# Weight chunks in the order of use, masks written by VectorE, and squares added by TensorE in a three-layer transformer kernel

## The chip, the cores and the metric

The kernel runs on one core of one Trainium2 chip. The metric is the device time of one execution in microseconds. The core's engines are named as the profile names them: PE (TensorE matmul) and PEld (its weight load), DVE (VectorE), ACT (ScalarE), POOL (GpSimd) and SP (SyncE, which issues most DMAs).

## The reference

A sequence of 256 tokens of width 1024 goes through one block with two kinds of softmax attention and then through two blocks with two feed-forward stages each, a mixer between them (retention in the first, stick-breaking attention in the second) and a gated embedding at the end. Everything is float32. Cut to what the change touches:

```python
def rms_norm(x, w):                       # also on the latents cq (384 wide) and ckv (256 wide)
    return x * rsqrt(mean(x * x, -1) + 1e-6) * w

def chunk_causal_attention(q, k, v, scale):     # 8 heads of one kind (two scores each), 8 of the other
    mask = key_chunk[None, :] <= q_chunk[:, None]      # chunks of 64 tokens, query blocks of 128
    sc = where(mask, einsum('bhqd,bhkd->bhqk', qi, k) * scale, -1e30)
    return softmax(sc) @ v

def stick_breaking(h, w_in, w_out):             # 8 heads, strictly causal
    z = q @ k.T * scale
    log_one_minus = where(kpos < qpos, log_sigmoid(-z), 0)
    rem = reversed_cumsum(log_one_minus) - log_one_minus
    a = where(kpos < qpos, exp(log_sigmoid(z) + rem), 0)
    return (a @ v) @ w_out

# the end of each of the two later blocks
gate = sigmoid(rmsnorm(h, g[6]) @ ple_w_gate[i])
h = h + rmsnorm(gate * (p[i] @ ple_w_proj[i]), g[7])
```

## The kernel before

**Precision.** Each float32 product with a weight is made of three products of rounded parts. `chunk` loads up to 2,048 columns of weights with one DMA into `w_raw`, ACT rounds each piece of 512 columns into `w_hi` (L191) and DVE writes the rest into `w_lo` (L192). There are twelve buffers of each. `mm3` (L200) then issues hi by hi, lo by hi and hi by lo. Activations lie in SBUF as a pair of the same kind (`x_hi`, `x_lo`, or `a_hi`, `a_lo` in the second half of a feed-forward stage), with features on the partitions.

**Weights by tokens.** In `tokens` a tile of 128 features by 128 tokens is the stationary operand and 512 weight columns stream past it. `parts` are the (usually two) column ranges, `groups` the runs of k (tiles of 128 features) that are worked off together, and `b` the two halves of 128 tokens. The loops run over group, b, part j, k. The chunks, though, are laid out with k outside and the part inside, so that the pieces of a group of four k stand as k0 j0, k0 j1, k1 j0, k1 j1 in the first chunk, and k2 and k3 in the second. All feed-forward stages, the output projections and the embedding's gate go this way. The other way round (`mat_steps`, L217), with weights stationary, serves the heads' projections.

**Heads.** In the first block the score matmuls of a head, its transposes and its value products stand between slices of other projections; numbers such as `FILL_DA` say how many filler matmuls go between. A scheduler orders the instructions of each engine within this, by priorities and by the lines `issue_after`. In `scores`, matmuls with a single-row operand `masks` (L665: `q0` is one for the first 64 queries, `k1` is -1e30 for the keys that they must not see) open the accumulation of each score tile S, and the products of q and k add to it (L672). A differential head has two tiles S with 64 rows of q and k each; the other kind of head (MLA) has one, from 128 rows `k,q` and 64 rows `kr,qr`. `softmax` then reads each S with a maximum on DVE (L682) and an exponential on ACT (L690). `ot` (L857) are the transposes of the preceding differential head's output, which depend on its normalisation on POOL and DVE.

**Latents.** `sumsq` adds the squares of the latents' tiles (three for cq, two for ckv): ACT squares, POOL adds into `acc` (L291), and two matmuls per latent with a column of ones sum `acc` over the partitions (L294).

**Stick-breaking.** `sums` builds reversed cumulative sums in `c` by six matmuls with `tri_r` and `ones_r`, and adds the mask by two more, `ident_r` by `neg_r` (L1218, L1221). DVE scales S into `zs` (L1199), and later adds c (L1222).

**Gated embedding.** `ple_gate` runs `tokens` over eight k in the groups `[0..3]` and `[4..7]`. When the last group's half b is done, ACT takes a tanh `z` (L1298), DVE multiplies into `e` (L1300), `residual` squares, scales by `r` (POOL, L302) and adds into `h` (L421). The next stage begins with `features`: PE transposes h into `xt` (L435), ACT and DVE write `x_hi` and `x_lo` (L439, L441). The line `issue_after(self.turn_at)` holds those transposes back until three `mm3` are left of the half that is being issued (`TURN_AT`). The first of the two embedding stages is followed by a feed-forward stage, the second ends the kernel.

Of the kernel before, what the change touches and what calls it, by code (L numbers as in the profile page):

```python
# [10 lines left out]
F32 = mybir.dt.float32  # L11
# [3 lines left out]
ALU = mybir.AluOpType  # L15
# [49 lines left out]
K_ID, K_F1, K_F2, NK = 0, 128, 129, 130  # L65
K_TRI, K_M01, K_NEG, NKS = 0, 128, 256, 384


def constants():

    i = np.arange(P)
    c = np.zeros((P, NK), np.float32)
    c[:, K_ID : K_ID + P] = np.eye(P)
    m = np.zeros((1, 4 * P), np.float32)
    m[0, :P] = i < 64
    for at in (192, 448):
        m[0, at : at + 64] = NEG
# [6 lines left out]
    t[:, K_NEG : K_NEG + P] = np.where(i[:, None] >= i[None, :], NEG, 0.0)  # L84
# [10 lines left out]
    return c, t, d, m  # L95

# [51 lines left out]
class Build:  # L148
# [93 lines left out]
    def tokens(self, parts, X, nk, banks, groups, before=(None, None)):  # L242

        width = sum(len(cols) for *_, cols in parts)
        starts = np.cumsum([0] + [len(cols) for *_, cols in parts]).tolist()
        per = CHUNK // width
        for g in groups:
            at = {}  # L250
            for i in range(0, len(g), per):
                W = self.chunk([(name, lead, k, cols) for k in g[i : i + per] for name, lead, cols in parts])
                at.update({k: (W, x * width) for x, k in enumerate(g[i : i + per])})
            for b in range(2):
                if g is groups[0] and before[b] is not None:
                    before[b]()
                left = len(parts) * len(g)
                for j, (*_, cols) in enumerate(parts):
                    for k in g:
                        left -= 1  # L260
                        W, c = at[k]
                        x = tuple(t[:, k, b * P : (b + 1) * P] for t in X)
                        self.mm3(banks[b][j], x, W(c + starts[j], len(cols)), k == groups[0][0], k == groups[-1][-1])
# [17 lines left out]
    def sumsq(self, n, tile):  # L281

        nc = self.nc
        ss = self.psa.tile([P, 2], F32, name="ss", tag="a")
        acc = self.tmp.tile([P, T], F32, name="acc", tag="acc", bufs=1)
        for i in range(n):
            src = tile(i)
            sq = acc if i == 0 else self.tmp.tile([P, T], F32, name="sq", tag="sq")
            nc.scalar.activation(sq, src, AF.Square)
            if i:  # L290
                nc.gpsimd.tensor_add(acc, acc, sq)  # L291
            yield i, src
        for b in range(2):
            nc.tensor.matmul(  # L294
                ss[:, b : b + 1], acc[:, b * P : (b + 1) * P], self.ones[:, 0:1],
                start=b == 0, stop=b == 1, skip_group_check=True,
            )
        self.ss = ss
# [242 lines left out]
    def setup_scores(self):  # L541
        nc, const, aps = self.nc, self.const, self.aps
        mk = self.tmp.tile([1, 4 * P], F32, name="mk", tag="sq")
        nc.gpsimd.dma_start(mk, aps["mk"])
        masks = self.rounded(const, "masks", mk)
        self.q0, self.k1 = masks[:, 0:P], masks[:, P:]

# [111 lines left out]
    def scores(self, Ss, parts):  # L659
# [3 lines left out]
        with self.at_pe():  # L663
            for S in Ss:
                mm(S, self.q0, self.k1, start=True, stop=False, skip_group_check=True)  # L665
            for b in range(2):
                at = slice(0, P) if b == 0 else slice(P, 3 * P)
                qs, ks = slice(b * P, (b + 1) * P), slice(0, (b + 1) * P)
                for n in range(len(parts[0])):
                    for S, qk in zip(Ss, parts):  # L670
                        q, k = qk[n]
                        mm(S[:, at], q[:, qs], k[:, ks], start=False, stop=n == len(parts[0]) - 1, skip_group_check=True)  # L672

    def softmax(self, Ss, scale):
# [4 lines left out]
        mx = self.sm.tile([P, 4], F32, name="mx", tag="mx", bufs=3)  # L679
        for e, S in enumerate(Ss):  # L680
            for b in range(2):
                nc.vector.tensor_reduce(mx[:, 2 * e + b : 2 * e + b + 1], S[:, cols[b]], axis=AX.X, op=ALU.max)  # L682
# [472 lines left out]
    def stick(self, X, R, before, row):  # L1155
        nc, tc = self.nc, self.tc
        spec = lambda c0: ("sb_w_in_2", (0,), range(c0, c0 + P))
        with tc.tile_pool(name="stick", bufs=1) as sp:
# [30 lines left out]
            def scores(h):  # L1189
# [8 lines left out]
                nc.scalar.activation(u, u, AF.Exp, scale=-1.0)  # L1198
                nc.vector.tensor_scalar_mul(zs, S, SB_SCALE)  # L1199
                nc.scalar.activation(u, u, AF.Ln, bias=1.0)  # L1200
# [8 lines left out]
            def sums(h):  # L1209
# [3 lines left out]
                with self.at_pe():  # L1213
                    mm(c[:, 0 : 2 * P], tri_r, lhi[:, 0 : 2 * P], start=True, stop=False)
                    mm(c[:, 0 : 2 * P], tri_r, llo[:, 0 : 2 * P], start=False, stop=False)
                    mm(c[:, P : 2 * P], ones_r, lhi[:, 2 * P :], start=False, stop=False)
                    mm(c[:, P : 2 * P], ones_r, llo[:, 2 * P :], start=False, stop=False)
                    mm(c[:, 0:P], ident_r, neg_r, start=False, stop=True)  # L1218
                    mm(c[:, 2 * P :], tri_r, lhi[:, 2 * P :], start=True, stop=False)
                    mm(c[:, 2 * P :], tri_r, llo[:, 2 * P :], start=False, stop=False)  # L1220
                    mm(c[:, 2 * P :], ident_r, neg_r, start=False, stop=True)  # L1221
                nc.vector.tensor_add(zs, zs, c)  # L1222
# [61 lines left out]
    def ple_gate(self, i, X, R, before, e, row, out):  # L1284
# [114 lines left out]
```

## Time and profile before

| | |
|---|---|
| median of three runs | 1623.23 us (1621.54 to 1623.61) |
| the profiled execution | 1622.01 us, its span 1620.2 us |
| PE busy | 1606.6 us, 99% of the span |
| DVE, ACT, POOL busy | 1061.3, 904.0, 90.1 us |
| granted TensorE clock, mean | 0.997 |
| DMA | 288.60 MB, mean 178 GB/s |

The rows of the profile read so: line of the kernel, engine, operation, output<-inputs, output and input shapes, count, then busy time and the mean duration of one in ns, then the engine's idle time before them and what ended it. A row of the timeline begins with the start and the duration in us; rows of equal instructions that follow each other are merged with a count, and idle time stands in brackets. A matmul's duration contains its way through the array, which overlaps the next one: what a matmul costs in a full stream is the distance from its start to the next start. A float32 matmul that isn't a transpose shows as two instructions, and the program's order below shows it as one.

### The profile page before, as it was taken

The numbers are of one execution on the slowest core, as the hardware profiler recorded it, in microseconds if no ns is written. First come the engines' busy times: TensorE is split into PE (matmuls) and PEld (weight loads), VectorE is DVE, ScalarE is ACT, GpSimd is POOL, SyncE is SP. The second block draws the span as 40 slices with busy tenths as digits, with TensorE's granted clock in tenths as the row PEclk, the third lists the DMA queues.
The fourth block names the chain that finished last, engine by engine and source line by source line (L and its number), as shares of the span: only waits on it lengthen the run. The fifth ranks groups of instructions, "written<-read, shape, count | busy, mean of one in ns | idle before, by whom it ended". The sixth has DMA issues, their size and how long they took to land.

```text
span 1620.2 us, 22387 instructions
## 1 busy us (share of the span) xinstructions
PE 1606.6 (99%) x8258; PEld 1349.5 (83%) x8258; DVE 1061.3 (66%) x1948; ACT 904.0 (56%) x1792; POOL 90.1 (6%) x101
## 2 busy tenths in 40 slices
PE   9999999999999999999999999999999999999997
PEld 9898778888888888898888888878888899888886
DVE  7987656755556555777766565576655677666546
ACT  7655544755455554645546555475554656655545
POOL 1100000200002000100000000030000200000002
PEclk9999999999999999999999999999999999999999
DMA  7535435555545555455455555555555453555451
GB/s 254 211 122 180 161 104 195 195 182 186 184 175 208 187 177 195 168 187 178 164 190 178 188 180 193 190 195 182 182 182 182 172 191 134 178 182 182 182 184 64
DMA packets 46862, 288.60 MB, mean 178 GB/s; under 512 B 5968, under 2 KB 9168, under 8 KB 13856
## 3 DMA queue, kind: packets, MB, share of 16 engines
q1 hardware_dynamic: 44240, 279.29, 48.7%
q0 software_dynamic: 2080, 7.67, 1.4%
q8 instruction: 65, 1.06, 0.3%
q14 instruction: 45, 0.37, 0.1%
q10 hardware_dynamic: 432, 0.20, 0.0%
HBM read 284.65 MB, written 1.05 MB: 176 GB/s over the span
## 4 chain that ended last, share of the span: by engine, by line
PE 95%; DVE 2%; DMA 1%; issue 1%; ACT 1%; SPq 0%; POOL 0%; POOLq 0%; DVEq 0%; ACTq 0%
PE ps L200 78%; PE ps L217 9%; PE at L638 1%; PE S L672 1%; PE xt L435 1%; DMA w_raw<-in_w 1%; DVE w_lo L192 1%; PE o L200 1%; PE o L713 0%; PE S L665 0%; PE S L1079 0%; PE S L1195 0%; DMA h<-in_x 0%; PE pt L703 0%; PE o L840 0%
## 5 line engine op out<-in xcount | busy, mean ns | idle before, releaser
L192 DVE TENSOR_TENSOR w_lo<-w_raw,w_hi 128x512 fp32r<-128x512 f32 x1054 | 707.5, 687 | 363.9 <-ACT w_hi L191 360.2
L191 ACT CAST w_hi<-w_raw 128x512 fp32r<-128x512 f32 x1054 | 638.7, 621 | 482.7 <-PE ps L200 355.3
L200 PE MATMUL ps<-w_hi,x_hi 128*128 128x512 f32 (+1 forms) x1280 | 489.4, 382 | 1.1 <-ACT x_hi L439 1.1
L200 PE MATMUL ps<-w_hi,x_lo 128*128 128x512 f32 (+1 forms) x1280 | 483.5, 378 | 1.2 <-DVE x_lo L441 1.2
L200 PE MATMUL ps<-w_lo,x_hi 128*128 128x512 f32 (+1 forms) x1280 | 482.4, 377 | 0.0
L200 PEld LDWEIGHTS ps<-w_hi,x_lo 128*128 128x128 f32 x1280 | 241.1, 188 | 47.3 <-DVE x_lo L441 2.4
L200 PEld LDWEIGHTS ps<-w_hi,x_hi 128*128 128x128 f32 x1280 | 241.3, 188 | 43.9 <-ACT x_hi L439 1.5
L200 PEld LDWEIGHTS ps<-w_lo,x_hi 128*128 128x128 f32 x1280 | 241.4, 189 | 42.0
L200 PE MATMUL ps<-w_hi,a_hi 128*128 128x512 f32 x440 | 176.8, 402 | 0.0
L200 PE MATMUL ps<-w_hi,a_lo 128*128 128x512 f32 x440 | 173.4, 394 | 0.0
L200 PE MATMUL ps<-w_lo,a_hi 128*128 128x512 f32 x440 | 172.6, 392 | 0.0
L302 POOL TENSOR_TENSOR r<-v,mhalf 128x1 f32<-128x1 f32 (+1 forms) x50 | 63.7, 1274 | 1239.8 <-DVE v L390 1100.6
L217 PE MATMUL ps<-x_hi,w_hi 128*128 128x256 f32 x440 | 114.7, 289 | 0.2 <-DVE h L780 0.2
L217 PE MATMUL ps<-x_hi,w_lo 128*128 128x256 f32 x440 | 112.5, 284 | 0.0
L200 PEld LDWEIGHTS ps<-w_hi,a_lo 128*128 128x128 f32 x440 | 82.6, 188 | 21.4
L200 PEld LDWEIGHTS ps<-w_lo,a_hi 128*128 128x128 f32 x440 | 82.7, 188 | 19.1
L200 PEld LDWEIGHTS ps<-w_hi,a_hi 128*128 128x128 f32 x440 | 82.7, 188 | 18.3
L217 PEld LDWEIGHTS ps<-x_hi,w_hi 128*128 128x128 f32 x440 | 84.1, 191 | 1.3 <-issue 0.7
L217 PEld LDWEIGHTS ps<-x_hi,w_lo 128*128 128x128 f32 x440 | 84.2, 192 | 0.6 <-DVE w_lo L192 0.3
L217 PE MATMUL ps<-x_lo,w_hi 128*128 128x256 f32 x440 | 77.5, 283 | 0.0
L633 DVE SCALAR_TENSOR_TENSOR a<-ps,R,s 128x512 f32<-128x512 f32 (+1 forms) x60 | 42.2, 703 | 52.2 <-PE ps L200 44.6
L274 ACT CAST a_hi<-at 128x512 fp32r<-128x512 f32 (+1 forms) x60 | 33.1, 552 | 67.9 <-PE at L638 67.9
(282 smaller groups left out, 1506.1 us busy)
## 6 DMA issues: line engine op xcount, KB each, us to landing
w_raw<-in_w SPq DMA_DIRECT2D x256, 1024.0 KB, 4.8
gr<-in_rows POOLq DMA_DIRECT2D x10, 512.0 KB, 4.6
w_raw<-in_w SPq DMA_DIRECT2D x12, 256.0 KB, 4.9
w_raw<-in_w SPq DMA_DIRECT2D x6, 384.0 KB, 3.2
w_raw<-in_w SPq DMA_DIRECT2D x3, 512.0 KB, 3.6
h<-in_x SPq DMA_DIRECT2D x4, 256.0 KB, 4.9
h<-in_x POOLq DMA_DIRECT2D x1, 1024.0 KB, 7.9
out<-h SPq DMA_DIRECT2D x3, 256.0 KB, 2.5
```

Source lines behind the costliest of these rows:

```text
L191: nc.scalar.copy(hi[:, :m], r[:, c0:c1])
L192: nc.vector.tensor_sub(lo[:, :m], r[:, c0:c1], hi[:, :m].bitcast(F32))
L200: mm = lambda a, b, **k: nc.tensor.matmul(ps, a, b, skip_group_check=True, **k)
L217: mm = lambda *a, **k: self.nc.tensor.matmul(*a, skip_group_check=True, **k)
L274: nc.scalar.copy(hi, src)
L302: self.nc.gpsimd.tensor_tensor(r, v, self.mhalf[:, :n], op=ALU.pow)
L435: nc.tensor.transpose(pt[:, i, :], self.h[:, b, k * P : (k + 1) * P], self.ident)
L633: nc.vector.scalar_tensor_tensor(a, banks[1], R[:, b : b + 1], s, op0=ALU.mult, op1=ALU.mult)
L638: nc.tensor.transpose(pt[:, i, :], a[:, i * P : (i + 1) * P], self.ident)
L672: mm(S[:, at], q[:, qs], k[:, ks], start=False, stop=n == len(parts[0]) - 1, skip_group_check=True)
```

## The change

It has four parts.

1. `tokens` lays a group's chunks out by part and then k, which is the order in which the matmuls use them.
2. The embedding's gate takes its eight k as three and five.
3. The masks leave PE. In the softmax heads the first product of q and k opens the accumulation, and a DVE memset (`masked`) writes -1e30 into the two 64 by 64 squares of S before the maximum is taken. In the stick-breaking heads the mask comes into `zs` where DVE scales S, from a constant that is now 384 columns wide, and the two matmuls with `neg_r` go.
4. `sumsq` keeps the squares of all tiles of a latent, and PE adds them: two matmuls for each tile instead of two for the sum. POOL's additions go.

```diff
     # tokens
-        width = sum(len(cols) for *_, cols in parts)
-        per = CHUNK // width
+        per = CHUNK // len(parts[0][2])
         for g in groups:
-            at = {}
-            for i in range(0, len(g), per):
-                W = self.chunk([(name, lead, k, cols) for k in g[i : i + per] for name, lead, cols in parts])
-                at.update({k: (W, x * width) for x, k in enumerate(g[i : i + per])})
+            at, order = {}, [(j, k) for j in range(len(parts)) for k in g]
+            for i in range(0, len(order), per):
+                part = order[i : i + per]
+                W = self.chunk([(*parts[j][:2], k, parts[j][2]) for j, k in part])
+                at.update({jk: (W, x * len(parts[0][2])) for x, jk in enumerate(part)})
     # sumsq
-        acc = self.tmp.tile([P, T], F32, name="acc", tag="acc", bufs=1)
+        sq = self.tmp.tile([P, 3, T], F32, name="sqs", tag="acc", bufs=1)
         for i in range(n):
             src = tile(i)
-            sq = acc if i == 0 else self.tmp.tile([P, T], F32, name="sq", tag="sq")
-            nc.scalar.activation(sq, src, AF.Square)
-            if i:
-                nc.gpsimd.tensor_add(acc, acc, sq)
+            nc.scalar.activation(sq[:, i, :], src, AF.Square)
             yield i, src
...
+        for i in range(n):
+            for b in range(2):
+                nc.tensor.matmul(
+                    ss[:, b : b + 1], sq[:, i, b * P : (b + 1) * P], self.ones[:, 0:1],
+                    start=i == b == 0, stop=i == n - 1, skip_group_check=True,
+                )
     # setup_scores
-        mk = self.tmp.tile([1, 4 * P], F32, name="mk", tag="sq")
-        nc.gpsimd.dma_start(mk, aps["mk"])
-        masks = self.rounded(const, "masks", mk)
-        self.q0, self.k1 = masks[:, 0:P], masks[:, P:]
     # scores
-            for S in Ss:
-                mm(S, self.q0, self.k1, start=True, stop=False, skip_group_check=True)
...
-                        mm(S[:, at], q[:, qs], k[:, ks], start=False, stop=n == len(parts[0]) - 1, skip_group_check=True)
+                        mm(S[:, at], q[:, qs], k[:, ks], start=n == 0, stop=n == len(parts[0]) - 1, skip_group_check=True)
+    def masked(self, S):
+        tail = S.rearrange("p (c n) -> p c n", n=64)
+        self.nc.vector.memset(tail[0:64, 1:6:4, :], NEG)
     # softmax
         for e, S in enumerate(Ss):
+            self.masked(S)
     # stick
-            neg_r = self.rounded(sp, "neg_r", ks[:, K_NEG : K_NEG + P])
-            ident_r = self.rounded(sp, "ident_r", self.ident)
-            m01 = ks[:, K_M01 : K_M01 + P]
+            m01, neg = ks[:, K_M01 : K_M01 + P], ks[:, K_NEG : K_NEG + 3 * P]
...
-                nc.vector.tensor_scalar_mul(zs, S, SB_SCALE)
+                nc.vector.scalar_tensor_tensor(zs, S, SB_SCALE, neg, op0=ALU.mult, op1=ALU.add)
...
-                    mm(c[:, 0:P], ident_r, neg_r, start=False, stop=True)
-                    mm(c[:, 2 * P :], ident_r, neg_r, start=False, stop=True)
     # ple_gate
-        groups = [list(range(0, 4)), list(range(4, 8))]
+        groups = [list(range(0, 3)), list(range(3, 8))]
```

The order of the instructions moves with it. On PE, at the scores of the third differential head (S with its two tiles, `ot` the transposes of the second-last head's output, `ps` filler), before:

```order
L217 MATMUL ps_1035<-x_lo_103,w_hi_1042 128x256 x2
L857 MATMUL ot_1078<-kc_84,oo_1014 128x128
L665 MATMUL S_1083<-masks_797 128x384
L857 MATMUL ot_1078<-kc_84,oo_1014 128x128
L665 MATMUL S_1084<-masks_797 128x384
L672 MATMUL S_1083<-k_901,q_900 128x128
L672 MATMUL S_1084<-k_901,q_900 128x128
L672 MATMUL S_1083<-k_901,q_900 128x256
```

and at the same place with the change:

```order
L214 MATMUL ps_1031<-x_lo_103,w_hi_1038 128x256 x2
L851 MATMUL ot_1074<-kc_84,oo_1010 128x128
L660 MATMUL S_1079<-k_897,q_896 128x128
L851 MATMUL ot_1074<-kc_84,oo_1010 128x128
L660 MATMUL S_1080<-k_897,q_896 128x128
L660 MATMUL S_1079<-k_897,q_896 128x256
```

The masks are gone, and the first product of the first tile has moved up between the two transposes, away from that of the second tile.

On PE, at the start of the first embedding gate, from the transposes of the second half's features on (`ps_10554` and `ps_10550` are outputs of half b = 0, `ps_10555` and `ps_10551` of b = 1), before:

```order
L435 MATMUL xt_10653<-kc_84,h_82 128x128 x4
L435 MATMUL xt_10658<-kc_84,h_82 128x128 x4
L200 MATMUL ps_10554<-w_hi_10571,x_hi_10545 128x512
L200 MATMUL ps_10554<-w_lo_10572,x_hi_10545 128x512
L200 MATMUL ps_10554<-w_hi_10571,x_lo_10546 128x512
L200 MATMUL ps_10554<-w_hi_10581,x_hi_10545 128x512
L200 MATMUL ps_10554<-w_lo_10582,x_hi_10545 128x512
L200 MATMUL ps_10554<-w_hi_10581,x_lo_10546 128x512
L200 MATMUL ps_10554<-w_hi_10589,x_hi_10545 128x512
L200 MATMUL ps_10554<-w_lo_10590,x_hi_10545 128x512
L200 MATMUL ps_10554<-w_hi_10589,x_lo_10546 128x512
L200 MATMUL ps_10555<-w_hi_10559,x_hi_10545 128x512
```

and now:

```order
L429 MATMUL xt_10635<-kc_84,h_82 128x128 x4
L197 MATMUL ps_10550<-w_hi_10573,x_lo_10542 128x512
L429 MATMUL xt_10640<-kc_84,h_82 128x128 x4
L197 MATMUL ps_10550<-w_hi_10577,x_hi_10541 128x512
L197 MATMUL ps_10550<-w_lo_10578,x_hi_10541 128x512
L197 MATMUL ps_10550<-w_hi_10577,x_lo_10542 128x512
L197 MATMUL ps_10551<-w_hi_10555,x_hi_10541 128x512
```

Nine matmuls stood between the transposes and the first use of the second half's features, and three or four stand there now; the transposes themselves come after as many matmuls of the stage as before.

On PE, at the end of the first embedding gate (`ps_10556` and `ps_10552` are its last outputs, `ps_10847` and `ps_10845` the first of the next feed-forward stage, xt the transposes of the first half's features), before:

```order
L200 MATMUL ps_10556<-w_hi_10737,x_lo_10546 128x512
L435 MATMUL xt_10887<-kc_84,h_82 128x128 x4
L200 MATMUL ps_10556<-w_hi_10745,x_hi_10545 128x512
L435 MATMUL xt_10892<-kc_84,h_82 128x128 x4
L200 MATMUL ps_10556<-w_lo_10746,x_hi_10545 128x512
L200 MATMUL ps_10556<-w_hi_10745,x_lo_10546 128x512
L200 MATMUL ps_10847<-w_hi_10853,x_hi_10842 128x512
```

and now:

```order
L429 MATMUL xt_10885<-kc_84,h_82 128x128 x4
L197 MATMUL ps_10552<-w_hi_10721,x_hi_10541 128x512
L429 MATMUL xt_10890<-kc_84,h_82 128x128 x4
L197 MATMUL ps_10552<-w_lo_10722,x_hi_10541 128x512
L197 MATMUL ps_10552<-w_hi_10721,x_lo_10542 128x512
L197 MATMUL ps_10552<-w_hi_10727,x_hi_10541 128x512
L197 MATMUL ps_10552<-w_lo_10728,x_hi_10541 128x512
L197 MATMUL ps_10552<-w_hi_10727,x_lo_10542 128x512
L197 MATMUL ps_10552<-w_hi_10731,x_hi_10541 128x512
L197 MATMUL ps_10552<-w_lo_10732,x_hi_10541 128x512
L197 MATMUL ps_10552<-w_hi_10731,x_lo_10542 128x512
L197 MATMUL ps_10845<-w_hi_10851,x_hi_10840 128x512
```

Behind the transposes stood three matmuls of the gate, and nine stand there now, before the next stage's first matmul asks for `x_hi`. Ahead of them stand 21 matmuls of the half b = 1 in both.

More of the change, by code (lines that the diff above doesn't have):

```diff
@@ L65 @@
 K_ID, K_F1, K_F2, NK = 0, 128, 129, 130
-K_TRI, K_M01, K_NEG, NKS = 0, 128, 256, 384
+K_TRI, K_M01, K_NEG, NKS = 0, 128, 256, 640
 def constants():
@@ L73, in constants @@
     c[:, K_ID : K_ID + P] = np.eye(P)
[L74 to L77, printed above, removed]
     base = (np.float64(10000.0) ** (np.arange(32) * (2 / 64))).astype(np.float32)
@@ L83, in constants @@
     t[:, K_M01 : K_M01 + P] = i[:, None] < i[None, :]
-    t[:, K_NEG : K_NEG + P] = np.where(i[:, None] >= i[None, :], NEG, 0.0)
+    for at in (K_NEG, K_NEG + 2 * P):
+        t[:, at : at + P] = np.where(i[:, None] >= i[None, :], NEG, 0.0)
     d = np.zeros((P, 4 * 256), np.float32)
@@ L94, in constants @@
         d[:, at + P : at + 2 * P] = zeta[:, None] * xi[None, :] / 16.0
-    return c, t, d, m
+    return c, t, d
 class Weights:
@@ L242, in tokens @@
     def tokens(self, parts, X, nk, banks, groups, before=(None, None)):
-        width = sum(len(cols) for *_, cols in parts)
-        starts = np.cumsum([0] + [len(cols) for *_, cols in parts]).tolist()
-        per = CHUNK // width
+        per = CHUNK // len(parts[0][2])
         for g in groups:
-            at = {}
-            for i in range(0, len(g), per):
-                W = self.chunk([(name, lead, k, cols) for k in g[i : i + per] for name, lead, cols in parts])
-                at.update({k: (W, x * width) for x, k in enumerate(g[i : i + per])})
+            at, order = {}, [(j, k) for j in range(len(parts)) for k in g]
[3 more added lines that the diff above has]
+                at.update({jk: (W, x * len(parts[0][2])) for x, jk in enumerate(part)})
             for b in range(2):
@@ L260, in tokens @@
                         left -= 1
-                        W, c = at[k]
+                        W, c = at[j, k]
                         x = tuple(t[:, k, b * P : (b + 1) * P] for t in X)
-                        self.mm3(banks[b][j], x, W(c + starts[j], len(cols)), k == groups[0][0], k == groups[-1][-1])
+                        self.mm3(banks[b][j], x, W(c, len(cols)), k == groups[0][0], k == groups[-1][-1])
                         if left == TURN_AT:
@@ L284, in sumsq @@
         ss = self.psa.tile([P, 2], F32, name="ss", tag="a")
-        acc = self.tmp.tile([P, T], F32, name="acc", tag="acc", bufs=1)
+        sq = self.tmp.tile([P, 3, T], F32, name="sqs", tag="acc", bufs=1)
         for i in range(n):
             src = tile(i)
-            sq = acc if i == 0 else self.tmp.tile([P, T], F32, name="sq", tag="sq")
-            nc.scalar.activation(sq, src, AF.Square)
-            if i:
-                nc.gpsimd.tensor_add(acc, acc, sq)
+            nc.scalar.activation(sq[:, i, :], src, AF.Square)
             yield i, src
[L293 to L297, printed above, removed]
+        for i in range(n):
[4 more added lines that the diff above has]
+                )
         self.ss = ss
@@ L541, in setup_scores @@
     def setup_scores(self):
-        nc, const, aps = self.nc, self.const, self.aps
-        mk = self.tmp.tile([1, 4 * P], F32, name="mk", tag="sq")
-        nc.gpsimd.dma_start(mk, aps["mk"])
-        masks = self.rounded(const, "masks", mk)
-        self.q0, self.k1 = masks[:, 0:P], masks[:, P:]
+        nc, const = self.nc, self.const
         lt = self.lam
@@ L1216, in sums @@
                     mm(c[:, P : 2 * P], ones_r, lhi[:, 2 * P :], start=False, stop=False)
-                    mm(c[:, P : 2 * P], ones_r, llo[:, 2 * P :], start=False, stop=False)
-                    mm(c[:, 0:P], ident_r, neg_r, start=False, stop=True)
+                    mm(c[:, P : 2 * P], ones_r, llo[:, 2 * P :], start=False, stop=True)
                     mm(c[:, 2 * P :], tri_r, lhi[:, 2 * P :], start=True, stop=False)
-                    mm(c[:, 2 * P :], tri_r, llo[:, 2 * P :], start=False, stop=False)
-                    mm(c[:, 2 * P :], ident_r, neg_r, start=False, stop=True)
+                    mm(c[:, 2 * P :], tri_r, llo[:, 2 * P :], start=False, stop=True)
                 nc.vector.tensor_add(zs, zs, c)
@@ L1382 @@
         "pos2": inputs["positions_2"],
-        **dict(zip(("kc", "ks", "kd", "mk"), constants())),
+        **dict(zip(("kc", "ks", "kd"), constants())),
     }
```

## The prediction

> **What bounds the kernel now.** I read the page's totals first, then the chain of work that ended last, then busy time by stage.
>
> ```profile
> PE 1606.6 (99%) x8258; PEld 1349.5 (83%) x8258; DVE 1061.3 (66%) x1948; ACT 904.0 (56%) x1792; POOL 90.1 (6%) x101
> ...
> PE 95%; DVE 2%; DMA 1%; issue 1%; ACT 1%; SPq 0%; POOL 0%; POOLq 0%; DVEq 0%; ACTq 0%
> ```
>
> PE is busy for 99% of the span and makes up 95% of the chain. A PE instruction that goes is therefore worth its distance to the next start, and cover given to another engine is worth something only where PE shows a wait. Two stretches, by stage (length, then busy time and count of PE, PEld, DVE, ACT, POOL, granted clock, DMA share, GB/s):
>
> ```profile
> 60.00:80.00 20.00, 20.00 (x118) 16.61 (x118) 19.70 (x51) 14.69 (x37) 0.69 (x1) 1.00 0.38 123
> 240.00:1080.00 840.00, 840.00 (x4122) 702.04 (x4122) 535.30 (x911) 458.17 (x858) 46.67 (x48) 1.00 0.52 185
> ```
>
> In the 840 us of output projections, feed-forward stages and retention PE never waits. In the first heads DVE is busy 19.70 of 20.00 us beside a full PE: that engine gets more work.
>
> **Masks off PE.** An MLA head at the output projection, and a retention head's scores, which have no mask ahead of them:
>
> ```profile
> 198.35 0.40 PE L200 MATMUL ps<-w_hi,oa_l 128*128 128x512 f32 x1
> 198.68 0.43 PE L665 MATMUL S<-masks 1*128 1x384 f32 x1
> 199.04 0.49 PE L672 MATMUL S<-k,q 128*128 128x128 f32 x2
> 199.46 0.49 PE L672 MATMUL S<-kr,qr 64*128 64x128 f32 x2
> 199.88 0.70 PE L672 MATMUL S<-k,q 128*128 128x256 f32 x2
> ```
>
> ```profile
> 705.73 0.40 PE L200 MATMUL ps<-w_hi,x_lo 128*128 128x512 f32 x1
> 705.96 1.47 PE L1079 MATMUL S<-q,k 128*128 128x256 f32 x8
> ```
>
> The step into the mask takes .33 us (198.35 to 198.68) and the step out of it .36; without a mask a 512-wide matmul hands over to a 128-row score in .23. So a mask ahead of 128-row scores is worth .33 + .36 - .23 = .46, not only its streaming. Eight MLA heads: 3.7 us.
>
> A differential head has 64-row scores, and its masks alternate with the 128-row transposes `ot`; the two first heads have no `ot`:
>
> ```profile
> 78.52 0.27 PE L857 MATMUL ot<-kc,oo 128*128 128x128 f32 x1
> 78.72 0.43 PE L665 MATMUL S<-masks 1*128 1x384 f32 x1
> 79.09 0.33 PE L857 MATMUL ot<-kc,oo 128*128 128x128 f32 x1
> 79.35 0.44 PE L665 MATMUL S<-masks 1*128 1x384 f32 x1
> 79.72 0.93 PE L672 MATMUL S<-k,q 64*128 64x128 f32 x8
> 80.57 0.39 PE L217 MATMUL ps<-x_hi,w_hi 128*128 128x256 f32 x1
> ```
>
> ```profile
> 56.04 0.61 PE L665 MATMUL S<-masks 1*128 1x384 f32 x2
> 56.58 0.93 PE L672 MATMUL S<-k,q 64*128 64x128 f32 x8
> ```
>
> From 78.52 to 80.57 is 2.05. The order with the change leaves `ot`, one score product, `ot`, the rest: .20 for the first `ot`, .42 for a 64-row product alone (priced by 199.46 to 199.88), .26 for the second `ot`, and .85 for the rest (79.72 to 80.57, kept whole, since the row doesn't tell what of it is the change of shape): 1.73. Gain .32 for each of six heads, 1.9. In the first two heads the pair of masks takes .54, 1.1 together.
>
> ```profile
> L665 PE MATMUL S<-masks 1*128 1x384 f32 x24 | 10.0, 428 | 0.0
> ```
>
> Those are all 24: 8 + 12 + 4. Sum 6.7. The bounds: if the changes between row counts stay and only 384 of 512 columns of .23 go, 24 x .17 = 4.1; at .37 each (78.72 to 79.09), 8.8. I take 6.7, because it follows neighbours in the same place.
>
> The Trainium skill (TensorEngine Tiling (Array Packing), Tiling Modes) says that changing the tiling mode drains TensorE. It speaks against this part: in the differential heads a 64-row product comes to stand between two 128-row transposes, so the change of mode would remain there, and by it only streaming would go in the 16 masks of these heads, 16 x .17 = 2.7 instead of 3.0. The trace agrees that such steps are dear (.33, .36 and .42 against .23); that is the first rival's mechanism.
>
> **Memsets on DVE.** The trace of before has none on S.
>
> ```profile
> L682 DVE TENSOR_REDUCE mx<-S 128x1 f32<-128x128 f32 x24 | 6.8, 285 | 7.5 <-PE S L672 7.5
> L684 DVE TENSOR_SCALAR nm<-mx 128x4 f32<-128x4 f32 x8 | 1.3, 164 | 0.1
> ```
>
> A small DVE operation takes .164, and one that reads 128 columns of S .285; 64 rows by 128 columns written lie between: some .2, so 24 give 4.8 us to DVE, ahead of the maximum and so ahead of the exponential and the value products. POOL and ACT get nothing. What hides it is the filler between a head's scores and its value products, and the lead of the twelve weight buffers. I cost it at nothing; a gain is excluded, since it is work added to an engine. With 19.70 of 20.00 used, that cover can run out; its price then is up to 24 x .285 = 6.8.
>
> **A longer wait for `oo`.**
>
> ```profile
> L857 PE MATMUL ot<-kc,oo 128*128 128x128 f32 x16 | 4.8, 298 | 0.5 <-DVE oo L850 0.5
> ```
>
> One `ot` of 16 waits: the last differential head's, ahead of MLA scores. PE comes there sooner by a mask and by products that now stand behind it, so the wait grows: +.4, between 0 and the .46 of a mask.
>
> **The mask in stick-breaking.**
>
> ```profile
> 1325.06 0.28 PE L1218 MATMUL c<-neg_r,ident_r 128*128 128x128 f32 x1
> 1325.18 0.27 PE L1219 MATMUL c<-lhi,tri_r 128*128 128x128 f32 x1
> ```
>
> ```profile
> L1199 DVE TENSOR_SCALAR zs<-S 128x384 f32<-128x384 f32 x8 | 4.4, 552 | 0.4 <-ACT u L1197 0.4
> L1222 DVE TENSOR_TENSOR zs<-zs,c 128x384 f32<-128x384 f32 x8 | 4.4, 545 | 0.0
> ```
>
> Such a matmul costs .12 or a little less; two for each of eight heads, 16 x .11 = 1.8 (0 if PE would only wait there for the next sums, 1.9 at .12). DVE's scaling gets a second tensor operand: of this size that takes .545 in L1222 against .552 in L1199, so nothing.
>
> **Squares by PE.**
>
> ```profile
> 50.42 0.61 PE L294 MATMUL ss<-ones,acc 128*128 128x1 f32 x4
> 50.88 0.37 PE L217 MATMUL ps<-x_hi,w_hi 128*128 128x256 f32 x1
> ```
>
> Two matmuls, four instructions, take .46. Five tiles instead of two sums are six matmuls more, 12 x .115 = +1.4; at most 1.6. POOL's additions were on nobody's path that PE shows, so their going earns nothing. The Trainium skill (TensorEngine Tiling (Array Packing), Performance Considerations) gives some 60 cycles of overhead to a matmul, however few its columns; an estimate from that, at 2.4 GHz, is 12 x .025 = .3, and the sum below would be 1.1 lower. The trace's .115 decides.
>
> **Chunks by part.** In the feed-forward stages weights are never late (840.00 of 840.00), and chunk count, bytes and SP's queue stay the same: nothing, at least nothing lost, as a part's first chunk now holds what PE asks for first.
>
> **Groups of three and five.** At a gate's start the half b = 0 gets 18 matmuls instead of 24, so six matmuls less, 6 x .23 = 1.4, cover the transposes of the other half's features. DVE has one `w_lo` less to write ahead of `x_lo` with the new order of chunks, so I take +.2 for both gates; the bound is 2 x 1.4 = 2.8. SP issues five weight DMAs for a gate instead of four, well ahead.
>
> At the end of the first gate PE does wait:
>
> ```profile
> 1086.56 0.39 PE L200 MATMUL ps<-w_hi,x_lo 128*128 128x512 f32 x1
> 1087.42 0.66 PE L435 MATMUL xt<-kc,h 128*128 128x128 f32 x4 [0.47 <-DVE h L421]
> ...
> 1090.32 0.50 PE L200 MATMUL ps<-w_hi,x_hi 128*128 128x512 f32 x1 [1.09 <-ACT x_hi L439]
> ...
> 1092.68 0.80 PE L200 MATMUL ps<-w_hi,x_lo 128*128 128x512 f32 x1 [1.17 <-DVE x_lo L441]
> ...
> 1095.96 0.48 PE L200 MATMUL ps<-w_hi,x_lo 128*128 128x512 f32 x1
> ```
>
> 1086.56 to 1095.96 is 9.40 us for 12 matmuls of .23 and 16 transposes of some .11, 4.6 us of work: 4.8 lost, 2.26 of it in the waits for `x_hi` and `x_lo`, the rest in the wait for h and in steps that are longer than .23 behind the waits. The last half's 30 matmuls instead of 24 put 1.4 between the end of b = 0 and the first use of its features. So 1.4 of the 2.26 goes, and with it some .5 of the slow steps; what is late next is `x_lo` still, and then h of b = 1, whose chain starts only with the gate's last matmul: -1.9 (0 to -4.8).
>
> At the kernel's end:
>
> ```profile
> 1611.49 0.39 PE L200 MATMUL ps<-w_hi,x_lo 128*128 128x512 f32 x1
> 1611.66 0.63 ACT L403 ACTIVATE sq<-e 128x512 f32<-128x512 f32 x1 [1.70 <-DVE e L1300]
> 1612.29 0.82 ACT L1298 ACTIVATE z<-ps,R 128x256 f32<-128x256 f32 x2
> ```
>
> The last matmul is through at 1611.88, but its tanh begins at 1612.29, behind the square of b = 0, which came late. With 1.4 more between the halves that square is done: -.4.
>
> **The sum.** -6.7 - 1.8 + 1.4 + .4 + .2 - 1.9 - .4 = -8.8. The profiled execution took 1622.01, so 1613.2; the median of the runs lies 1.2 above it, so 1614.4.
>
> **The rivals.** First, switches stay: row counts still change at the scores, and only the masks' streaming goes, 4.1 instead of 6.7. The .42 of the 64-row product speaks for it, the .23 of retention against it where 128-row scores follow. 1614.4 + 2.6 = 1617.0.
>
> Second, the group of three starves: the start costs 2.8 instead of .2, and the end gains nothing, because the chain of b = 1 decides it. For it speak the waits at 1090.32 and 1092.68, which show that features take longer than a few matmuls; against it, that DVE has less ahead of them. 1614.4 + 2.6 + 1.9 = 1618.9.
>
> Third, DVE is full in the first heads and each memset delays a head's value products: +6.8, 1621.2, no difference.
>
> Fourth, the slow one: the stationary tile matters to the pace of the stream. `masks` goes from the constants, and tiles behind it move.
>
> ```profile
> L200 PE MATMUL ps<-w_hi,x_hi 128*128 128x512 f32 x1120 | 443.4, 396 | 1.1 <-ACT x_hi L439 1.1
> L200 PE MATMUL ps<-w_hi,a_hi 128*128 128x512 f32 x440 | 176.8, 402 | 0.0
> ```
>
> The same matmul takes 396 ns from one tile and 402 from another. If the moved x took on that pace, 3 x 1120 x 6 ns = 20 us, 1634; from 12 us, 3.6 ns each, it would decide against all the rest. The durations are modelled and mixed of stages, which speaks against it.
>
> **How the numbers follow.** A measurement of this kernel can tell about 0.2%, 3.2 us. Chances: the sum .58, switches .21, the group of three .1, DVE .07, pace .04. The forecast is the likeliest, 1614.4. Its own range, by the bounds of masks (4.1 to 8.8) and of the gate's end, is 1610.5 to 1617; with the first two rivals it is 1610.5 to 1619, which leaves out the last two and some of the tails. Faster than 1620.0: the first three, less a tail, .87. Within: DVE and that tail, .09. Slower: .04.
>
> **What would show it.** Right: 24 fewer matmuls of `masks`, with .23 from a 512-wide matmul to an MLA score; three steps of some .4 around `ot`; no new wait for `p`; less than 1 us of waits for `x_hi` and `x_lo` at the first gate's end; a wait under .3 at each gate's start. Wrong: waits of PE for `p` or for weights between 40 and 240 us, a wait for the second half's `x_hi` or `x_lo` behind 18 matmuls, or a 512-wide stream whose step isn't .23.

## The result and the profile after

The changed kernel took 1613.68 us (median of four runs, 1612.93 to 1614.39) against 1622.63 (1621.54 to 1623.61): a ratio of 0.9939, 95% interval 0.9926 to 0.9951. That is 9.0 us less; 8.8 from a median of 1623.23 had been forecast. One execution, of the kernel with the squares back on POOL further down, took 2243.36 us at a granted clock of .656 and stands in none of the figures here. The span of its profiled execution is 1611.5 us, 8.7 less than before. Totals, the chain's engines, and the same two stretches by stage:

```profile
PE 1597.7 (99%) x8230; PEld 1344.3 (83%) x8230; DVE 1065.2 (66%) x1969; ACT 904.1 (56%) x1792; POOL 79.9 (5%) x97
PE 95%; DVE 2%; DMA 1%; issue 1%; ACT 1%; SPq 0%; POOL 0%; POOLq 0%; DVEq 0%; ACTq 0%
60.00:80.00 20.00, 20.00 (x125) 17.33 (x123) 19.74 (x56) 14.34 (x37) 0.69 (x1) 1.00 0.39 138
240.00:1080.00 840.00, 840.00 (x4122) 702.17 (x4121) 537.49 (x911) 459.61 (x859) 40.26 (x49) 1.00 0.53 185
```

PE is still the bound at 99%, and has lost 8.9 us of busy time. DVE has 3.9 more, and is as full as before in the first heads (19.74 of 20.00). An MLA head and the third differential head, on PE's timeline:

```profile
196.96 0.40 PE L197 MATMUL ps<-w_hi,oa_l 128*128 128x512 f32 x1
197.20 0.38 PE L660 MATMUL S<-k,q 128*128 128x128 f32 x2
197.52 0.48 PE L660 MATMUL S<-kr,qr 64*128 64x128 f32 x2
197.93 0.70 PE L660 MATMUL S<-k,q 128*128 128x256 f32 x2
198.56 0.70 PE L660 MATMUL S<-kr,qr 64*128 64x256 f32 x2
199.19 0.51 PE L197 MATMUL ps<-w_hi,oa_h 128*128 128x512 f32 x1
```

```profile
79.76 0.27 PE L851 MATMUL ot<-kc,oo 128*128 128x128 f32 x1
79.96 0.48 PE L660 MATMUL S<-k,q 64*128 64x128 f32 x2
80.38 0.33 PE L851 MATMUL ot<-kc,oo 128*128 128x128 f32 x1
80.64 0.92 PE L660 MATMUL S<-k,q 64*128 64x128 f32 x6
81.49 0.38 PE L214 MATMUL ps<-x_hi,w_hi 128*128 128x256 f32 x1
```

The step into the MLA scores is .24 instead of .33, and the block from S's first matmul to the next weight product 1.99 instead of 2.45 (198.68 to 201.13 before). The differential block is 1.73 long, as the sum had put together from other rows (.20, .42, .26, .85), instead of 2.05. The memsets, and the one wait of PE that grew in the heads (in all, times, longest):

```profile
L665 DVE MEMSET S<- 64x128 f32 x24 | 3.8, 165 | 4.0 <-PE S L660 3.7
PE ot L851 <- DVE oo L844: 0.9, 1, 0.9
```

Stick-breaking's sums, and the two sums of squares (12 and 8 instructions, each with the next weight product's start):

```profile
1317.96 0.27 PE L1209 MATMUL c<-llo,ones_r 128*128 128x128 f32 x1
1318.07 0.28 PE L1210 MATMUL c<-lhi,tri_r 128*128 128x128 f32 x1
1318.18 0.28 PE L1211 MATMUL c<-llo,tri_r 128*128 128x128 f32 x1
1318.30 0.33 PE L214 MATMUL ps<-x_hi,w_hi 128*128 128x256 f32 x1
```

```profile
48.18 1.40 PE L288 MATMUL ss<-ones,sqs 128*128 128x1 f32 x12
49.44 0.36 PE L214 MATMUL ps<-x_hi,w_hi 128*128 128x256 f32 x1
...
52.39 0.94 PE L288 MATMUL ss<-ones,sqs 128*128 128x1 f32 x8
53.20 0.36 PE L214 MATMUL ps<-x_hi,w_hi 128*128 128x256 f32 x1
```

The first gate's end, and the kernel's end:

```profile
1081.66 0.66 PE L429 MATMUL xt<-kc,h 128*128 128x128 f32 x4 [0.48 <-DVE h L415]
...
1085.14 0.50 PE L197 MATMUL ps<-w_hi,x_hi 128*128 128x512 f32 x1 [0.29 <-ACT x_hi L433]
...
1086.89 0.50 PE L197 MATMUL ps<-w_hi,x_lo 128*128 128x512 f32 x1 [0.55 <-DVE x_lo L435]
```

```profile
1602.68 0.39 PE L197 MATMUL ps<-w_hi,x_lo 128*128 128x512 f32 x1
1603.17 0.84 ACT L1288 ACTIVATE z<-ps,R 128x256 f32<-128x256 f32 x2 [0.93 <-PE ps L197]
```

The waits for `x_hi` and `x_lo` fall from 1.09 and 1.17 to .29 and .55, together by 1.42, which is what six matmuls of .23 cover. The last tanh starts .49 instead of .80 behind the last matmul's start.

Both traces have 7,284 weight products on PE (output `ps`). Setting the start of the n-th of one against that of the n-th of the other, at places where the orders agree, shows where the time went:

| Stretch, by the time before | Forecast, us | Measured, us |
|---|---|---|
| start to 24.5 | 0 | +1.2 |
| sums of squares, to 52.4 | +1.4 | +1.1 |
| differential heads, to 166 | -3.0 | -3.5 |
| MLA heads and the wait for `oo`, to 241 | -3.3 | -3.4 |
| feed-forward stages, retention, gate's start, to 1085 | +.1 | +.1 |
| first gate's end, to 1098 | -1.9 | -2.6 |
| stick-breaking, to 1388 | -1.8 | -1.9 |
| the rest of the stream, to 1611.5 | +.1 | +.1 |
| last matmul to the end of the span | -.4 | +.1 |

The columns add up to -8.8 and, unrounded, -8.7. The score blocks by themselves, each from the matmul ahead of it to the next filler, are 3.0 shorter in the differential heads and 4.0 in the others, the longer wait included; the rest of those two rows lies between the blocks. Two rows need an explanation that these two traces can't give: the start, where the change touches nothing, and the .7 too much at the gate's end.

### The profile page after: what moved, and what is told of

The parts are those of the page before. It is cut to its first block, busy times and chain, and to the rows that moved or that the text cites. A ratio compares the mean times of both kernels' runs of the same rounds, so it can differ in the third digit from the quotient of the medians.

```text
span 1611.5 us, 22515 instructions
## 1 busy us (share of the span) xinstructions
PE 1597.7 (99%) x8230; PEld 1344.3 (83%) x8230; DVE 1065.2 (66%) x1969; ACT 904.1 (56%) x1792; POOL 79.9 (5%) x97
## 3 DMA queue, kind: packets, MB, share of 16 engines
q8 instruction: 64, 1.05, 0.3%
HBM read 284.78 MB, written 1.05 MB: 177 GB/s over the span
## 4 chain that ended last, share of the span: by engine, by line
PE 95%; DVE 2%; DMA 1%; issue 1%; ACT 1%; SPq 0%; POOL 0%; POOLq 0%; DVEq 0%; ACTq 0%
PE ps L197 78%; PE ps L214 9%; PE at L628 1%; PE S L660 1%; PE xt L429 1%; DMA w_raw<-in_w 1%; DVE w_lo L189 1%; PE o L197 1%; PE o L707 0%; DMA h<-in_x 0%; PE S L1073 0%; PE S L1187 0%; PE pt L697 0%; PE o L834 0%; PE ot L1110 0%
```

## The experiments

Eleven kernels were run, one of them twice. Times are medians. The kernel before, measured beside them, took 1623.1 us beside the kernels without the memsets, with the first version of another order, with four and four and with two and six; beside all others it took 1622.6.

**Masks alone.** The kernel before with part 3's softmax half only:

```diff
-            for S in Ss:
-                mm(S, self.q0, self.k1, start=True, stop=False, skip_group_check=True)
...
+            self.masked(S)
```

> The kernel before, with only the masks moved from PE to DVE memsets. Theory (a mask costs its streaming and the changes of row count around it, the memset is hidden): between the first head and the last PE gains 6.7 us, so about 1616 us. Rival (row counts change anyway, only streaming goes): 4.1 us less, about 1618.5. Rival (memsets delay the heads): no difference, and waits of PE for p or for the exponential's results between 55 and 240 us.

1615.57 us, ratio 0.9957 (0.9945 to 0.9969): 7.1 less, the first theory's figure. That is most of the change's gain. No wait of PE for `p` appeared in its trace; the waits for `oo` add up to 1.4 there (.52 and .86), where the kernel before has .51.

**A mask of 128 rows.** Here the masks stay on PE and stream as many columns; only their operand becomes 128 rows high:

```diff
-        mk = self.tmp.tile([1, 4 * P], F32, name="mk", tag="sq")
-        nc.gpsimd.dma_start(mk, aps["mk"])
+        mk = self.tmp.tile([P, 4 * P], F32, name="mk", tag="sq")
+        nc.vector.memset(mk, 0.0)
+        nc.gpsimd.dma_start(mk[0:1, :], aps["mk"])
```

> The kernel before, with the mask's operand as 128 rows, 127 of them zero, instead of one row; it streams the same 384 columns. Theory (the change of row count is what makes a mask dear): at an MLA head the step from a 512-wide matmul into the mask falls from .33 to .23, and the step out of it from .36 to about .2; beside the differential heads' ot the steps of .37 fall to about .2, while the step from the last mask to the 64-row products stays near .4. In all 2 to 3.5 us less, 1619 to 1620.5. Rival (a mask is dear because it is a single-pass start of an accumulation, whatever its rows): the steps stay at .33 to .37, no difference.

1616.07 us, ratio 0.9964 (0.9952 to 0.9977): 6.6 less, with all 24 masks in place. An MLA head and a differential head of it:

```profile
196.99 0.39 PE L200 MATMUL ps<-w_hi,oa_l 128*128 128x512 f32 x1
197.22 0.34 PE L666 MATMUL S<-masks 128*128 128x384 f32 x1
197.39 0.38 PE L673 MATMUL S<-k,q 128*128 128x128 f32 x2
197.70 0.48 PE L673 MATMUL S<-kr,qr 64*128 64x128 f32 x2
...
199.37 0.50 PE L200 MATMUL ps<-w_hi,oa_h 128*128 128x512 f32 x1
```

```profile
112.66 0.27 PE L858 MATMUL ot<-kc,oo 128*128 128x128 f32 x1
112.69 0.42 PE L666 MATMUL S<-masks 128*128 128x384 f32 x1
112.94 0.27 PE L858 MATMUL ot<-kc,oo 128*128 128x128 f32 x1
112.97 0.42 PE L666 MATMUL S<-masks 128*128 128x384 f32 x1
113.32 0.93 PE L673 MATMUL S<-k,q 64*128 64x128 f32 x8
114.18 0.38 PE L217 MATMUL ps<-cq_h,w_hi 128*128 128x256 f32 x1
```

The step into the mask is .23 (was .33), the step out .17 (was .36): what a mask of 128 rows costs ahead of 128-row scores is its streaming. Where the row count still changes, from the last mask to the 64-row products, the step is .35 (was .37). The differential block is 1.52 long, shorter than the changed kernel's 1.73 though it has two masks more, because here the 64-row products stand together behind 128-row work. So it was the change of row count, not the 384 columns, that made the masks dear, and the second theory falls. By its blocks the kernel gains 6.3, more than the 2 to 3.5 that the first theory reckoned. In its profile PE gives 1.7 of that back in two waits, 1.05 ahead of the first head for `masks`, whose load now starts behind DVE's clearing, and .65 for `oo`. That profile is of the slowest of the five executions (1618.34); three took 1615.99 to 1616.07, and no trace shows what they did better. The Trainium skill (TensorEngine Tiling (Array Packing), Tiling Modes) says that a change of tiling mode drains TensorE; the trace agrees, with .1 to .2 at each change here.

**Without the memsets.** `self.masked(S)` is taken out of the changed kernel, so that it leaves out the mask of the softmax heads.

> The changed kernel without the 24 memsets (the keys of the later chunk are then not masked in the softmax heads). Theory (the memsets are hidden behind the filler between scores and value products): the same time as the changed kernel within 1 us, about 1613.7, and score blocks on PE of the same length. Rival (DVE is the bound of the first heads, and each memset delays them): up to 6.8 us less, about 1607 to 1610.

1613.31 us (1612.16 to 1613.91) against the changed kernel's 1613.68: the same. Its differential block is 1.73 long, and its 1,105th weight product starts at 236.49, the changed kernel's at 236.45. From the 169th to the 1,105th, all heads among them, it takes 204.57, the changed kernel 205.04, and the two with other groups, which have the memsets, 204.71 and 204.96. So 24 memsets of .165, 3.8 in all, are hidden, but for .1 to .5, behind the filler even where DVE is 99% busy. The third rival is out.

**Another order of the scores.** Two edits in the changed kernel, which follow from the rows above: the first holds the score products back behind both transposes, the second takes the `k,q` products of both query blocks ahead of the `kr,qr` products.

```diff
     # da_features
-                    nc.tensor.transpose(pt[:, b * P : (b + 1) * P], oo[:, b, :], self.ident)
+                    self.behind = nc.tensor.transpose(pt[:, b * P : (b + 1) * P], oo[:, b, :], self.ident).ins
     # scores
-            for b in range(2):
...
-                for n in range(len(parts[0])):
+            for n in range(len(parts[0])):
+                for b in range(2):
```

> The changed kernel with the score matmuls in another order: both transposes ot ahead of the score products (so that the two 64-row tiles' products stay side by side), and in an MLA head the two k,q products ahead of the two kr,qr products. Theory (each change between 128 rows and 64 rows costs, and two 64-row products side by side run together): a differential score block falls from 1.72 to about 1.2 (six heads, -3.3), an MLA block from 1.98 to about 1.7 (eight heads, -1.6 to -3); 1607 to 1609. Rival (only the streams count): the blocks keep their lengths, 1613.7. Rival (PE comes sooner to oo and waits there): one wait longer, up to +.5.

1607.93 us, ratio 0.9907 (0.9893 to 0.9920). In this version the second query block's start of the accumulation stands between the first block's two products, and the first block's scores in the MLA heads lack a product. With the start at the first product only (`start=n == b == 0`) both are added:

> The same order as in a4_order (transposes ahead, then products in the order k,q, k,q, kr,qr, kr,qr), with one start of the accumulation for each score tile instead of one for each part, so that all products are added. Theory: blocks on PE as in a4_order, 1.17 for a differential head and 1.60 for an MLA head, 1607 to 1609, 5 to 6 us less than the changed kernel. Rival (what a4_order gained came from products that were overwritten): blocks as in the changed kernel, 1613.7.

1607.67 us, ratio 0.9907 (0.9891 to 0.9924), 6.0 less than the changed kernel. Its differential block and its MLA block:

```profile
79.81 0.38 PE L851 MATMUL ot<-kc,oo 128*128 128x128 f32 x2
80.12 0.93 PE L660 MATMUL S<-k,q 64*128 64x128 f32 x8
80.98 0.39 PE L214 MATMUL ps<-x_hi,w_hi 128*128 128x256 f32 x1
...
200.71 0.82 PE L660 MATMUL S<-k,q 128*128 128x128 f32 x4
201.46 0.92 PE L660 MATMUL S<-kr,qr 64*128 64x128 f32 x4
202.31 0.38 PE L214 MATMUL ps<-cq_h,w_hi 128*128 128x256 f32 x1
```

1.17 instead of 1.73, and 1.60 instead of 1.99: the same instructions, in another order. Six times .56, six times .39, and .24 and .48 in the two heads between make 6.4, and longer waits for `oo` and in the filler take some of it back. The eight instructions of the two 64-row tiles take .86 side by side, while two of one tile alone took .42 in the changed kernel. The Trainium skill (TensorEngine Tiling (Array Packing), Tiling Modes) says that different tiles can multiply in parallel; the trace agrees: the differential head's four products, 768 columns of two tiles, take .86, and the MLA head's two `kr,qr` products, 384 columns of one tile, take .85 (201.46 to 202.31).

**The groups alone.** The kernel before with groups of three and five, the chunks as they were.

> The kernel before, with only the groups of three and five k in the embedding's gates, the chunks laid out as before. Theory: the first gate's end gains what the changed kernel shows there, about 2.5 us, and the waits for x_hi and x_lo fall from 1.09 and 1.17 to .3 and .55; about 1620. Rival (the order of the chunks is needed for it, since two w_lo lie on DVE ahead of x_lo at a gate's start): a new wait of up to 1.4 us for the second half's x_lo or for weights at each gate's start, so 1620 to 1623.

1620.77 us, ratio 0.9989 (0.9980 to 0.9998): 1.9 less in the medians. Waits of .29 and .55 stand at the gate's end, as in the changed kernel, and none at a gate's start. The order of the chunks isn't needed for it.

**Four and four in the changed kernel**, so that only the order of the chunks is left of the parts 1 and 2:

> The changed kernel with the embedding's groups as four and four k, so with the chunks by part but not the other groups. Theory: the first gate's end is as before the change, with waits of 1.1 and 1.2 for x_hi and x_lo, +2 to +2.5, about 1616. Rival (the order of the chunks brought the gain): 1613.7, waits as in the changed kernel.

1615.94 us (1614.14 to 1617.07), 2.3 more than the changed kernel, with waits of 1.10 and 1.17 again. It also answers for the .7: from the 4,881st to the 4,926th weight product its gate's end takes 15.96 us, and with the same groups 15.95 in the kernel with the masks alone and 15.98 in that with stick-breaking and squares alone (below). In the kernel before it took 16.99, in that with 128 rows 17.14; with three and five, and `features` as they are, it takes 14.38 to 14.41 in every execution. Over 15 us from there, in the kernel before and in that with the masks alone (length, busy time of the engines, granted clock, DMA share, GB/s):

```profile
1081.10:1096.10 15.00, 12.27 (x54) 9.38 (x53) 12.92 (x27) 12.54 (x33) 1.46 (x2) 0.89 0.33 126
1075.20:1090.20 15.00, 12.25 (x58) 8.96 (x57) 12.92 (x27) 13.67 (x38) 1.46 (x2) 1.00 0.32 119
```

The waits are the same in both. The granted clock was .89 in one and 1.00 in the other; in the kernel before it was .50 from 1092.4, in the wait for `x_lo`, to 1095.8, and the steps there show it:

```profile
1093.28 0.63 PE L200 MATMUL ps<-w_hi,x_hi 128*128 128x512 f32 x1
1093.70 0.63 PE L200 MATMUL ps<-w_lo,x_hi 128*128 128x512 f32 x1
```

This step is .42; the kernel with the masks alone takes .24 for the same one (1087.13 to 1087.37). So the groups are worth 1.55 there (15.95 less 14.40), and 1.0 of the 2.6 in the table is a dip of the clock in the profiled execution of before.

**Two and six**, to see whether more cover gives more:

> The changed kernel with the embedding's groups as two and six k. Theory: at the first gate's end the remaining waits for x_hi (.29) and x_lo (.55) go, since 1.4 us more of matmuls lie there, -.8 to -1.0; at each gate's start the first x_lo of the second half, which in the changed kernel is written about .2 us before it is read, comes some 1.2 us too late, +2.4; together about 1615. Rival (the transposes come earlier too, so that the start loses nothing): 1612.8.

1615.70 us (1614.16 to 1616.59), 2.0 more than the changed kernel. The theory failed at both places. Nothing waits at the gates' starts. At the end PE no longer waits for h, but the wait for `x_hi` is as it was (.28): `issue_after(self.turn_at)` holds the transposes back to the last nine matmuls of the half, however long the half is, so `x_hi` gets no more cover. The wait for `x_lo` is four times as long; DVE's rows show why:

```profile
1082.49 3.09 DVE L189 TENSOR_TENSOR w_lo<-w_raw,w_hi 128x512 fp32r<-128x512 f32 x5
...
1087.43 0.34 DVE L435 SCALAR_TENSOR_TENSOR x_lo<-xt,vecs,x_hi 128x128 fp32r<-128x128 f32 x1
1087.82 0.50 PE L197 MATMUL ps<-w_hi,x_lo 128*128 128x512 f32 x1 [2.35 <-DVE x_lo L435]
```

The scheduler put five pieces of weights, a later one and the gate's own `e` and `og` ahead of the first `x_lo`. With four and four and with three and five the place of `x_lo` in that queue is another. Cover on PE helps only if the engines that make the operand take it up sooner.

**Features ahead of weights.** The new order of the scores with a higher priority for the instructions of `features`:

```diff
-        with self.urgent():
+        with self.tc.high_priority(300):
```

> a6_order2 with the features' instructions ahead in the scheduler, so that x_hi and x_lo stand ahead of some w_hi and w_lo on ACT and DVE at the ends of the stages. Theory (the waits left at the first gate's end, .3 and .55, are those of x_hi and x_lo behind weight pieces in their engines' queues): both go, -.5 to -1 there. Rival (the weight pieces that are put back are late then): a new wait for w_hi or w_lo at the start of a stage, no difference or slower.

1606.27 us (1606.04 to 1606.80), ratio to the kernel before 0.9899 (0.9885 to 0.9914), the fastest here. The wait for `x_hi` at the first gate's end is as long as it was, .28. That for `x_lo` is gone there (a step of .35 without a wait), but a new one stands ahead of stick-breaking, where the other kernels have none:

```profile
1079.63 0.50 PE L197 MATMUL ps<-w_hi,x_lo 128*128 128x512 f32 x1
...
1275.35 0.50 PE L197 MATMUL ps<-w_hi,x_lo 128*128 128x512 f32 x1 [0.43 <-DVE x_lo L435]
```

From the 4,881st to the 4,950th weight product it takes 19.14 us instead of 19.88 with the new order of the scores alone, so .7 is gained at the gate's end, as the theory had it, through one of the two waits. From the 5,700th to the 5,800th it takes 25.56 instead of 24.96, and .6 is lost again. So at these two places the higher priority nets .1 of the 1.4 us between the two medians. In the profiles another .4 lies in the feed-forward stages and retention between the 1,201st and the 4,701st (771.11 against 771.50); why, and where the rest lies, stays open.

**The mask in stick-breaking and the squares**, on the kernel before:

> The kernel before, with only the stick-breaking mask in DVE's scaling and the squares added by PE. Theory: -1.8 us in the eight stick-breaking heads, +1.2 to +1.4 us at the two sums of squares (six matmuls, twelve instructions of .11 to .12); together about -.5, not to be told from no change in the time, but in the trace, place by place. Rival for the squares (with POOL's additions gone the latents' norms come earlier, and PE gains more than it pays): 0 or less at the sums. Rival for the mask (PE would only wait for the next operand): 0 in the stick-breaking heads.

1621.65 us, ratio 0.9995 (0.9987 to 1.0004), which can't be told from no change. In its trace the eight stick-breaking heads take 1.9 less, and the two sums 1.1 to 1.2 more, as in the changed kernel.

**Squares back on POOL**, with the new order of the scores:

> a6_order2 with the squares added by POOL again, as before the change. Theory (12 more instructions of .1 on PE are the whole cost of that part): 1.0 to 1.2 us less than a6_order2 at the two sums of squares, visible in the trace, about 1606.5 to 1607.5. Rival (POOL's additions of 2.3 us delay the latents' norms, now that heads are shorter): PE waits for the latents' features ahead of their first products, no difference or slower.

1606.65 us (1606.62 to 1607.38, three executions), 1.0 less than with PE's squares (1607.23 to 1607.82); the ranges overlap. That is the size that was expected, but not for the reason given. POOL's last addition and the sum behind it, in this kernel; then POOL's addition in the kernel before, which no row above showed:

```profile
49.48 2.73 POOL L287 TENSOR_TENSOR acc<-acc,sq 128x256 f32<-128x256 f32 x1 [13.14 <-ACT acc L285]
52.26 0.61 PE L290 MATMUL ss<-ones,acc 128*128 128x1 f32 x4 [1.13 <-POOL acc L287]
```

```profile
48.12 2.24 POOL L291 TENSOR_TENSOR acc<-acc,sq 128x256 f32<-128x256 f32 x1 [9.52 <-ACT acc L289]
```

Here PE waits 1.13 for POOL. Before, POOL was through at 50.36, and PE came at 50.42, so the addition was not late, but with .06 to spare. From the 169th to the 433rd weight product, the sums among them, this kernel and that with PE's squares gain .51 and .57 on the changed one: even. Their profiles are 1.2 apart: .6 lies ahead of that, at the start, and most of the rest behind it, in waits for `t` (.26) and `oo` (.39) that only the kernel with PE's squares has. No run ties these to the squares.

**The start.** One more execution of the new order of the scores:

> A second look at a6_order2, to tell what differs between two executions of one program: theory, the first 200 us (first weights, waits for x_hi and h) differ by 1 to 2 us, and the feed-forward stages not at all.

1607.46 us. Its 131st weight product starts at 25.29, in the first execution at 25.16, and from there to the end the two stay within .23 of each other: these two don't show the 1 to 2 us of the theory. Another pair does. The kernel before and that with the groups alone give PE, DVE, ACT and POOL the same instructions in the same order up to the first gate, 1,067 us into the span, yet their 131st weight products start at 24.48 and 25.75. So the +1.2 (24.48 to 25.64) is no more than two executions of the same instructions can differ. Over all fourteen profiles that start lies between 24.48 and 25.75; the kernel before happens to have the earliest. By the 1,105th weight product that pair is 3.4 apart, 1.3 of it from a clock of .50 between 196.9 and 200.3 in the kernel with the groups alone. From the 1,201st to the 4,701st weight product the kernel before and the changed one take 771.49 and 771.60 us.

## Why the prediction was right

The forecast was 8.8 us less, and the runs gave 9.0. By its steps:

- **Masks** with the wait for `oo`: -6.7 and +.4 forecast, -6.9 in the table, -7.0 by the blocks. That a mask costs the changes of row count around it was right, and the 128-row mask shows it. Undersized was only the MLA head: .55 instead of .46 (2.45 and .33 against 1.99 and .24), because the sum kept the .42 behind `k,q`, which is .32 now that no single row stands ahead.
- **Memsets**: nothing, right; .165 each, the lower bound.
- **The wait for `oo`**: +.4, and it went from .5 to .9; in other kernels without masks on PE such waits add up to .4 to 1.4.
- **Chunks by part**: nothing, right; 771.49 and 771.60 over the feed-forward stages and retention.
- **Stick-breaking**: -1.8, right, 1.9.
- **Squares**: +1.4 forecast, 1.1 in the table and 1.24 by the sums themselves (1.26 and .81 against .36 and .47): twelve instructions at .10, not .115. The step's second half, that POOL's additions earn nothing, was right for that execution only; they were .06 us from holding PE up.
- **Groups**: +.2 at the starts and -1.9 at the end; measured 0 and -1.55 (by executions at a granted clock of 1.00). The cover of 1.4 was exact. The .5 for the slow steps was the wrong term: steps of .42 behind the wait for `x_lo` come from a dip of the clock, which two of the five executions with these waits show.
- **Kernel's end**: the tanh came .3 sooner, as reckoned, and the last store landed 7.59 behind the last matmul's start instead of 7.84. But the span ended 1.28 behind that landing instead of .91, so it shows none of it.

With -7.0 for the masks and the wait, -1.9, +1.2 and -1.55 the measured terms add up to some -9.2, against 9.0 in the medians. In the two traces the 1.0 gained on the clock and the 1.2 lost at the start are both matters of one execution and nearly cancel. In the forecast the masks were .7 too small and the squares .2 too dear, and against that the kernel's end was .5 and the gates .15 too large. That the total is within .2 is partly luck.

The rival that switches stay was half right. They stay in the differential heads: `ot`, S, `ot`, S costs .42 and .26 there, and the time for it was in the sum. That the group of three starves, that DVE is full, and that the pace follows the tile were each shown wrong: no wait at a gate's start, the same time without the memsets, and 771.49 against 771.60 us.

## What to carry to other kernels

Ahead of a matmul of few rows, look at the row count of its neighbours on PE: a change costs .1 to .2 us each way, which for short products is more than their columns. Put products of equal row count together, and 64-row products of two tiles side by side; that was worth 6.0 us here at no cost, two thirds of what the whole change brought.

A wait for an operand is only as short as the place of its producer in that engine's queue allows: read the queue of ACT and DVE ahead of the wait before giving PE more cover, and look at the other stages afterwards: a higher priority took one wait for `x_lo` away here and made another elsewhere.

Before explaining .5 us between two traces, compare a stretch that nothing touched, and the granted clock at the place: two traces of the same instructions were 3.4 us apart here after 240 us.

## What the hardware showed that was not expected

- In three of the fourteen profiles the granted clock stood at .50 for 3.4 us in the middle of the stream: at the first gate's end in two of the five executions that have the two long waits there (.89 and .90 over 15 us), and at 196.9 us in the kernel with the groups alone, after a wait of .53 for `oo`. Other executions with the same waits kept 1.00. Each dip cost 1.0 to 1.3 us.
- A mask of 128 rows, 127 of them zeros, is .40 us cheaper at an MLA head than one of a single row (.23 + 2.15 against .33 + 2.45).
- The three additions of 128 by 256 numbers on POOL took .75, 2.24 and 3.87 us in the kernel before and .75, 1.14 and 2.73 in the kernel with the squares back on POOL. The last of each, at the second sum, took 2.24 and 2.73, where PE had .06 to spare.
